# First stage of a hybrid encoder block in another written order: meta tokens' norm ahead, norm row by a selector made on chip, first tile scaled in halves

## The chip, the core and the metric

The kernel runs on one core of a Trainium2 chip. The time is the device's time of one launch, in microseconds (us); the kernel before was run three times for it. A core has engines with a queue each, and every queue is worked off in order: TensorE (PE: matmuls, with PEld its loads of the stationary operand), VectorE (DVE), ScalarE (ACT), GpSimd (POOL) and SyncE (SP). Engines wait for each other by semaphores only. DMAs are issued from the queues of SP and ACT; an issue holds its place in that queue until what it waits for is there.

## The reference, cut to what matters

1024 tokens of 1024 float32 values, with 16 learned meta tokens ahead of them, go through one layer: a norm, a wide projection into eight parts, a pooling branch and a gated linear attention, both joined by gates, then a squared-ReLU MLP and a last norm. The change lies in the norm and in the part `v` of the projection.

```python
def rmsnorm(x, g):
    return x * lax.rsqrt(jnp.mean(x * x, axis=-1, keepdims=True) + EPS) * g

h = jnp.concatenate([meta, x], axis=1)
z = jnp.einsum('bld,dn->bln', rmsnorm(h, norm_mix[l]), w_in)
a, q, k, v, r, lr, ga, gb = jnp.split(z, IN_SPLITS, axis=-1)
```

## The kernel before, in words

**Arithmetic.** Most products are made of three float32r matmuls: each operand is split into a high part (ACT writes a rounded copy) and a low part (DVE subtracts it), and hi x hi, hi x lo and lo x hi go into one PSUM bank (`mm3`, lines 276 to 281). Each of the many products therefore needs an ACT and a DVE step on both of its operands.

**The first stage** (`first_stage`, with the functions that it defines) takes the tokens in tiles of 128 (t = 0 to 7; t = 8 is the 16 meta tokens). For each tile:

- `load` brings it in (`xs`, four slots; an SP DMA).
- `square`, `log`, `exp` (ACT) and `root` (four small DVE steps) make one factor for each token from the sum of squares.
- `scale` (line 498, DVE, 128x1024) multiplies by that factor and by the norm row `gB` into `us`. A `scale` also issues the load of a later tile. `gB` holds the 1024 values of `norm_mix` on all 128 partitions; it is made on chip before any `scale`.
- `turn t j` (line 513, PE) transposes half j of the tile, four 128x128 blocks, into a PSUM bank, `b_sc` and `b_ms` by turns. The two banks called `b_sc` are halves of one tile, `sc`.
- `hi` (line 526, ACT) and `lo` (line 529, DVE) split that half into `th` and `tl`; `keep` (line 519, ACT) copies it unsplit into `xr`. For tile 0, `keep` comes first and `hi`, `lo` read `xr`.
- `high i j` (line 541, ACT) and `low i j` (line 545, DVE) split half j of the weights' columns i = 0 or 1, that lie in `raw` and go to `vw`. `ask` issues the load of the next half of weights (SP); it waits until the old one in that buffer has been read. `low20` is a small piece of 16 columns.
- `value i t j` (PE) multiplies half j of tile t with weights i: twelve matmuls of 256 columns (272 for i = 1). Only for (0, 0) it uses the unsplit `xr` and raw weights, four float32 matmuls (line 382). `out i t` (line 399, ACT) takes the sum from its bank and stores it.
- `meta8` transposes the scaled meta tokens `um` (line 272, PE) and splits them; `value080` to `value181` use them.

On ACT, DVE, SP and PE of this stage, the order is written out by hand, as a list of words in `ORDER_1` (lines 418 to 430): `square0 log0 exp0 ...` calls `square(0)`, `log(0)` and so on, and each call's instructions go to the end of their engines' queues. PE's order is kept to the end of the program.

**Ahead of the list** stand the DMAs and the norm row. `ident` (a unit matrix) is loaded from ACT's queue; `norm_mix` follows it into eight partitions of `row`, which DVE has zeroed (line 449). Two `warm` matmuls of 128x512 on zeros come first on PE (line 467, each as two passes), then eight matmuls of 128 columns that use a column of `ident`, broadcast, to spread the eight pieces of the row over all partitions (line 474), DVE copies the two banks to `gB` (line 477), and three more `warm` follow.

**After the first stage** come the small gate projection (`lr_turn`, which needs `lrtok` of all tiles), pooling, the attention, the output projection and the MLP, the last two with seven products instead of eight for each 2x2 of blocks. Sums of blocks of `xr` for them (lines 701 to 705, DVE) already stand in DVE's queue at the end of the first stage. `W1` is the ring of weight blocks of the later projections; `W1.ask` (the word `wait00`) issues its two first loads, `W1.split` (`first1`, `first2`) splits them (lines 84 and 85).

Of the kernel before, what the change touches and what calls it, by code (L numbers as in the profile page):

```python
# [11 lines left out]
ALU = mybir.AluOpType  # L12
AX = mybir.AxisListType

P = 128
D = 1024
SEQ = 1024
META = 16
KT = D // P
# [103 lines left out]
def kernel(  # L123
# [3 lines left out]
    nc = tc.nc  # L127
    x = x[0]
    out = out[0]
# [73 lines left out]
    TH, TL = [], []  # L203
# [161 lines left out]
    def halves():  # L365
        return [slice(h * HALF, (h + 1) * HALF) for h in range(2)]
# [2 lines left out]

    v_bank = {}  # L370

    def v_half(i, t, j):
# [4 lines left out]
        if j == 0:  # L377
            v_bank[i, t] = bank("mm")
        b = v_bank[i, t][:n, :w]
        if (i, t) == (0, 0):  # L380
            for k in range(4 * j, 4 * j + 4):
                pe.matmul(b, S["xr"][:, k, :P], S["vraw"][j][:, k % 4], start=k == 0, stop=k == KT - 1)
        else:
            mm3(
                b, 4, lambda k: (TH[half][:, 4 * j + k, at : at + n], TL[half][:, 4 * j + k, at : at + n]),
                lambda k: (vw[:, 0, 4 * j + k], vw[:, 1, 4 * j + k]), first=j == 0, last=j == 1,
            )

    def v_out(i, t):
# [12 lines left out]
    def lr_turn():  # L402
# [13 lines left out]


    ORDER_1 = """
        square0 log0 exp0 root0 square1 scale0 log1 exp1 turn00 high00 root1 turn01 keep00 scale1 keep01 value000
        hi00 low00 ask10 high01 turn10 square2 low01 turn11 value001 ask11 hi10 log2 lo10 exp2 square3 root2 value010 scale2  # L420
        hi11 hi01 log3 lo11 out00 turn20 exp3 turn21 hi20 root3 value011 high10 lo20 scale3 high20 hi21 low20 value020 keep10
        keep11 lo01 square4 lo21 turn30 turn31 lo00 hi30 value021 log4 lo30 hi31 keep30 lo31 value030 exp4 keep20 out01
        root4 high11 low10 value031 out02 keep21 square5 scale4 value100 low11 wait00 log5 out03 exp5 turn40 turn41 root5
        value101 hi40 scale5 lo40 hi41 lo41 keep31 keep40 value110 out10 keep41 square6 log6 exp6 value111 value120
        out11 turn50 turn51 root6 hi50 scale6 lo50 hi51 lo51 value121 out12 value040 keep50 keep51 first1 value041 out04
        value130 turn60 turn61 hi60 lo60 hi61 lo61 value131 out13 square7 log7 exp7 root7 scale7 value050 keep60 keep61
        value051 out05 value140 turn70 turn71 hi70 lo70 hi71 lo71 value141 out14 square8 log8 exp8 root8 scale8 value060
        keep70 keep71 value061 out06 first2 value150 meta8 value151 out15 value070 value071 out07 value160 value161 out16
        value170 value171 out17 value080 value081 out08 value180 value181 out18
    """  # L430

    def first_stage(xs, us, xm, um, lrraw):
# [7 lines left out]
        def load(t):  # L440
            nc.sync.dma_start(xs[:, t % 4], x[t * P : (t + 1) * P, :])
# [8 lines left out]
        nc.scalar.dma_start(row[:KT], norm_mix.rearrange("(k c) -> k c", c=P))  # L450
        act.preload_act_table_set("natural_log_exp_and_others")
        pool.memset(blank, 0.0)
# [12 lines left out]
        def warm(n, cols=HALF):  # L465
            for _ in range(n):
                pe.matmul(bank("ms")[:, :cols], blank[:, HALF:], blank[:, :cols], start=True, stop=True)

        warm(2)
        for h, c in enumerate(halves()):  # L470
            b = bank("mm")
            for i in range(4):
                k = 4 * h + i
                pe.matmul(
                    b[:, i * P : (i + 1) * P], ident[:, k : k + 1].broadcast_to([P, P]), row, start=True, stop=True
                )
            dve.tensor_copy(gB[:, c], b)
        warm(3)

        def square(t):  # L480
            act.activation(um[: P if t < 8 else META], x_in(t), ACT.Square, accum_out=cell(3, t))
# [7 lines left out]
        def root(t):  # L489
# [3 lines left out]
            dve.tensor_scalar(m, m, -0.5, 1.5, ALU.mult, ALU.add)  # L493
            dve.tensor_tensor(ss, y, m, ALU.mult)

        def scale(t):
            u = x_out(t)
            dve.scalar_tensor_tensor(u, x_in(t), cell(3, t), gB[: u.shape[0]], ALU.mult, ALU.mult)
            if t == 0:
                load(4)  # L500
# [42 lines left out]
        def low(i, j):  # L543
            whole, hi, lo = parts(i, j)
            dve.tensor_tensor(lo, whole, f32(hi), ALU.subtract)

        does = dict(
            wait=lambda i, j: W1.ask(),
            square=square, log=log, exp=exp, root=root, scale=scale, turn=turn, keep=keep, hi=hi, lo=lo, high=high,
            low=low, ask=ask, value=v_half, out=v_out, first=W1.split, meta=lambda t: transposed(um[:META], 0, 0),  # L550
        )
        for word in ORDER_1.split():
            name = word.rstrip("0123456789")
# [1166 lines left out]
```

## Time and profile before

| | |
|---|---|
| median of 3 runs | 1215.61 us (1215.55 to 1216.33) |
| the profiled execution's own time | 1216.04 us |
| its span on the core | 1214.3 us |
| PE busy | 1198.8 us (99%) |
| DVE busy | 841.8 us (69%) |
| ACT busy | 573.3 us (47%) |
| POOL busy | 77.7 us (6%) |

The profile is of one execution of its own; about 1.7 us of that execution's time lie around the span. Times in rows are microseconds from the span's start. A row of the timeline has start, duration, engine, line, operation, what it writes `<-` what it reads, shape, and how many instructions it merges; in brackets the idle time of the engine ahead of it and what ended it. Matmuls are pipelined: the next one starts before the one before has ended, so that an end is the start plus a little more than the pace. `xN` of a float32 matmul counts its passes, two for each instruction. A row of windows has for each engine the busy time and the number of instructions in that stretch.

### The profile page before, as it was taken

To read this page: it belongs to the slowest core of one execution; us is meant where nothing else is said; L and a number is where in the kernel's file an instruction comes from. 1 tells how busy PE (TensorE), PEld (TensorE's weight loads), DVE (VectorE), ACT (ScalarE), POOL (GpSimd) and SP (SyncE) were. 2 spreads that over 40 slices of the span, in tenths; PEclk is the share of its full clock that TensorE was granted. 3 is DMA by queue.
4 is the path that set the end of the run, shared out by engine and by line. 5 is a ranking of instruction groups with operands and counts; after the bars stand their busy time and mean duration, and the time that the engine had idled before them with its cause. 6 is when DMAs were issued, how large, how long until landed. Compare 5 with 4: busy or idle time off the path is not lost.

```text
span 1214.3 us, 18327 instructions
## 1 busy us (share of the span) xinstructions
PE 1198.8 (99%) x6775; PEld 993.0 (82%) x6775; DVE 841.8 (69%) x1386; ACT 573.3 (47%) x1013; POOL 77.7 (6%) x97
## 2 busy tenths in 40 slices
PE   9999999999999999999999999999999999999997
PEld 7999877877778887888788888888888888888886
DVE  7646567575777669726887667676675887887786
ACT  7537444444456224305655545454554444444544
POOL 0000053323230000000000000000000000000000
PEclk9999999999999999999999999999999999999999
DMA  8214243434338967812245444454479973333532
GB/s 241 78 53 130 89 120 123 145 124 141 119 111 287 336 219 254 302 40 87 87 144 169 146 157 157 130 171 145 162 245 307 353 235 100 96 97 94 174 96 87
DMA packets 151385, 192.79 MB, mean 159 GB/s; under 512 B 12216, under 2 KB 86256, under 8 KB 151296
## 3 DMA queue, kind: packets, MB, share of 16 engines
q1 hardware_dynamic: 151136, 191.56, 49.1%
q8 instruction: 53, 0.87, 0.3%
q14 instruction: 36, 0.29, 0.1%
q10 hardware_dynamic: 160, 0.07, 0.0%
HBM read 128.66 MB, written 62.93 MB: 158 GB/s over the span
## 4 chain that ended last, share of the span: by engine, by line
PE 88%; DVE 5%; DMA 3%; issue 2%; ACT 1%; POOL 0%; SPq 0%; DVEq 0%; ACTq 0%; POOLq 0%
PE b_mm L279 7%; PE b_mm L280 7%; PE b_mm L281 7%; PE b_y L279 6%; PE b_y L280 6%; PE b_y L281 6%; PE b_oa L279 5%; PE b_oa L281 5%; PE b_oa L280 5%; PE b_z L279 4%; PE b_z L280 4%; PE b_z L281 4%; PE b_sc L279 4%; PE b_ob L279 4%; PE b_ob L280 4%; PE b_ob L281 4%
## 5 line engine op out<-in xcount | busy, mean ns | idle before, releaser
L768 ACT ACTIVATE w1h<-raw 128x512 fp32r<-128x512 f32 x106 | 65.9, 623 | 57.8 <-PE b_y L280 23.2
L769 DVE TENSOR_TENSOR w1l<-raw,w1h 128x512 fp32r<-128x512 f32 x106 | 72.5, 685 | 20.4 <-ACT w1h L768 20.4
L279 PE MATMUL b_sc<-th,w1h 128*128 128x512 f32 x216 | 85.6, 396 | 0.6 <-ACT u2p L1503 0.6
L279 PE MATMUL b_z<-th,w1h 128*128 128x512 f32 x216 | 85.3, 395 | 0.5 <-DVE c L887 0.3
L280 PE MATMUL b_sc<-tl,w1h 128*128 128x512 f32 x216 | 84.9, 393 | 0.0
L280 PE MATMUL b_z<-tl,w1h 128*128 128x512 f32 x216 | 84.2, 390 | 0.4 <-DVE tl L1389 0.4
L281 PE MATMUL b_sc<-th,w1l 128*128 128x512 f32 x216 | 84.4, 391 | 0.0
L768 ACT ACTIVATE w1h<-fs 128x512 fp32r<-128x512 f32 x81 | 51.1, 631 | 70.3 <-PE b_y L280 33.3
L281 PE MATMUL b_z<-th,w1l 128*128 128x512 f32 x216 | 84.1, 389 | 0.0
L769 DVE TENSOR_TENSOR w1l<-fs,w1h 128x512 fp32r<-128x512 f32 x81 | 56.9, 703 | 26.6 <-ACT w1h L768 26.5
L279 PE MATMUL b_mm<-th,w1h 128*128 128x512 f32 (+1 forms) x208 | 72.0, 346 | 0.0
L281 PE MATMUL b_mm<-th,w1l 128*128 128x512 f32 (+1 forms) x208 | 71.1, 342 | 0.0
L280 PE MATMUL b_mm<-tl,w1h 128*128 128x512 f32 (+1 forms) x208 | 71.0, 342 | 0.0
L768 ACT ACTIVATE w1h<-bt 128x512 fp32r<-128x512 f32 x46 | 29.1, 632 | 70.9 <-issue 43.9
L1579 DVE TENSOR_TENSOR bt<-w,w 128x512 f32<-128x512 f32 x80 | 54.7, 683 | 2.5 <-DMA w<-in_w_ff_dram 2.5
L279 PE MATMUL b_mm<-wo,th 128*128 128x512 f32 x128 | 50.3, 393 | 0.0
L281 PE MATMUL b_mm<-wo,tl 128*128 128x512 f32 x128 | 49.9, 390 | 0.0
L280 PE MATMUL b_mm<-wo,th 128*128 128x512 f32 x128 | 49.8, 389 | 0.0
L279 PE MATMUL b_y<-wo,w1h 128*128 128x512 f32 x128 | 49.8, 389 | 0.0
L280 PE MATMUL b_y<-wo,w1h 128*128 128x512 f32 x128 | 49.8, 389 | 0.0
L281 PE MATMUL b_y<-wo,w1l 128*128 128x512 f32 x128 | 49.8, 389 | 0.0
L769 DVE TENSOR_TENSOR w1l<-bt,w1h 128x512 fp32r<-128x512 f32 x46 | 31.8, 691 | 25.6 <-ACT w1h L768 25.6
(420 smaller groups left out, 3322.8 us busy)
## 6 DMA issues: line engine op xcount, KB each, us to landing
hf_dram<-h SPq DMA_DIRECT2D x112, 256.0 KB, 2.1
raw<-hf_dram SPq DMA_DIRECT2D x112, 256.0 KB, 2.7
w<-in_w_ff_dram SPq DMA_DIRECT2D x64, 256.0 KB, 4.6
raw<-in_w_in_dram SPq DMA_DIRECT2D x22, 512.0 KB, 4.5
raw<-in_w_ff_dram SPq DMA_DIRECT2D x16, 512.0 KB, 4.1
rawx<-in_w_ff_dram SPq DMA_DIRECT2D x16, 512.0 KB, 4.1
rawp<-in_w_in_dram SPq DMA_DIRECT2D x10, 512.0 KB, 4.4
xs<-in_x_dram SPq DMA_DIRECT2D x8, 512.0 KB, 4.9
```

The lines of the kernel that those rows point to most:

```text
L279: pe.matmul(ps, ah, bh, start=first and i == 0, stop=False, skip_group_check=more)
L280: pe.matmul(ps, ah, bl, start=False, stop=False, skip_group_check=more)
L281: pe.matmul(ps, al, bh, start=False, stop=last and i == n - 1, skip_group_check=more)
L768: act.activation(hi, a, ACT.Copy)
L769: dve.tensor_tensor(lo, a, f32(hi), ALU.subtract)
L1579: dve.tensor_tensor(bt, w, S["w2"][q[3:]][:, i], ALU.add if q[2] == "+" else ALU.subtract)
```

## The change

Five things are changed, all in the first stage.

1. **Norm row.** `norm_mix` is loaded as four rows of 256 into partitions 0, 32, 64 and 96 of a zeroed row buffer of 256 columns. Instead of a column of `ident`, four selectors of 128x128 are made on chip: DVE zeroes `ones` (128x512) and sets one partition of each to 1. Four matmuls of 256 columns (two `spread`) take the place of the eight of 128; `copy0` and `copy1` (DVE) are words of the list now. The DMA of `ident` moves from the head of ACT's queue to the third place of SP's, behind the first two tiles of tokens and ahead of the weights.
2. **Warm matmuls.** One 128x512 ahead of the spreads instead of two; four of 128x128 (`warm4`) behind `exp1` instead of three of 128x512.
3. **Tile 0** is scaled in two halves (`half00`, `half01`, 128x512 each).
4. **Quarters.** `bit i t q` multiplies a quarter (two of the eight blocks); `value011` and `value021` are written as `bit012 bit013` and `bit022 bit023`, with other work between them.
5. **The list.** Among other moves: `copy1 half00 half01` stand ahead of `root1`; `lo11` stands ahead of `root2 scale2`; `keep10 keep11` ahead of `hi20`; `lo21` ahead of `scale3`; `hi00 hi01 lo00 lo01` and `low11` ahead of `scale4`; `wait00` comes after `out10`; `square8 log8 exp8 root8 scale8`, the norm of the meta tokens, moves from behind `out14` to the words around `scale7`.

Three places, as each engine's queue has them. First ACT from the `log` of tile 3 on (line 484 before, 491 now): `th<-b_sc` and `th<-b_ms` are `hi` of tile 2, `th<-xr` is `hi` of tile 0, `xr<-b_sc` and `xr<-b_ms` the `keep` of tiles 1 and 2. Before:

```order
L484 ACTIVATE small<-small 128x1
L399 ACTIVATE vo<-b_mm 128x256
L487 ACTIVATE small<-small 128x1
L526 ACTIVATE th_132<-b_sc 128x4x128
L541 ACTIVATE vw_190<-raw_116 128x4x256
L541 ACTIVATE vw_190<-lrraw 128x8x16
L526 ACTIVATE th_132<-b_ms 128x4x128
L519 ACTIVATE xr<-b_sc 128x4x128
L519 ACTIVATE xr<-b_ms 128x4x128
L481 ACTIVATE um,small<-xs 128x1024
```

Now:

```order
L491 ACTIVATE small<-small 128x1
L494 ACTIVATE small<-small 128x1
L399 ACTIVATE vo<-b_mm 128x256
L530 ACTIVATE xr<-b_sc 128x4x128
L530 ACTIVATE xr<-b_ms 128x4x128
L537 ACTIVATE th_132<-b_sc 128x4x128
L537 ACTIVATE th_132<-b_ms 128x4x128
L399 ACTIVATE vo<-b_mm 128x256
L552 ACTIVATE vw_190<-raw_116 128x4x256
L552 ACTIVATE vw_190<-lrraw 128x8x16
```

Two `keep` stand between the bookkeeping of tile 3 and `hi20` now, where before `hi20` came at once and the two `keep` of tile 1 stood four rows below it. In the program the first of these `keep` waits for the last transpose of `turn20`, because both halves of `b_sc` are one tile.

Second DVE from the low half of `lrraw` to the scaling of tile 4 (`us<-xs`, line 498 before, 511 now); `tl` rows are `lo`, `vw_190` rows are `low`. Before:

```order
L545 TENSOR_TENSOR vw_190<-lrraw,vw_190 128x8x16
L529 TENSOR_TENSOR tl_136<-xr,th_132 128x4x128
L529 TENSOR_TENSOR tl_136<-b_ms,th_132 128x4x128
L529 TENSOR_TENSOR tl_136<-xr,th_132 128x4x128
L529 TENSOR_TENSOR tl_136<-b_sc,th_132 128x4x128
L529 TENSOR_TENSOR tl_136<-b_ms,th_132 128x4x128
L491 TENSOR_SCALAR small<-small 128x1
L492 SCALAR_TENSOR_TENSOR small<-small 128x1
L493 TENSOR_SCALAR small<-small 128x1
L494 TENSOR_TENSOR small<-small 128x1
L545 TENSOR_TENSOR vw_190<-raw_116,vw_190 128x4x256
L498 SCALAR_TENSOR_TENSOR us<-xs,small,gB 128x1024
```

Now:

```order
L556 TENSOR_TENSOR vw_190<-lrraw,vw_190 128x8x16
L556 TENSOR_TENSOR vw_190<-raw_116,vw_190 128x4x256
L540 TENSOR_TENSOR tl_136<-b_sc,th_132 128x4x128
L540 TENSOR_TENSOR tl_136<-b_ms,th_132 128x4x128
L540 TENSOR_TENSOR tl_136<-xr,th_132 128x4x128 x2
L498 TENSOR_SCALAR small<-small 128x1
L499 SCALAR_TENSOR_TENSOR small<-small 128x1
L500 TENSOR_SCALAR small<-small 128x1
L501 TENSOR_TENSOR small<-small 128x1
L556 TENSOR_TENSOR vw_190<-raw_120,vw_190 128x4x256
L511 SCALAR_TENSOR_TENSOR us<-xs,small,gB 128x1024
```

Now `low11` (`raw_120`) stands ahead of the scaling of tile 4; before it stood behind it.

Third DVE around the norm of the meta tokens (shapes with 16 partitions). Before:

```order
L529 TENSOR_TENSOR tl_144<-b_ms,th_140 128x4x128
L394 COPY lrtok<-b_mm 128x16
L491 TENSOR_SCALAR small<-small 16x1
L492 SCALAR_TENSOR_TENSOR small<-small 16x1
L493 TENSOR_SCALAR small<-small 16x1
L494 TENSOR_TENSOR small<-small 16x1
L701 TENSOR_TENSOR xr<-xr 128x4x512
L498 SCALAR_TENSOR_TENSOR um<-xm,small,gB 16x1024
```

Now:

```order
L498 TENSOR_SCALAR small<-small 16x1
L499 SCALAR_TENSOR_TENSOR small<-small 16x1
L500 TENSOR_SCALAR small<-small 16x1
L501 TENSOR_TENSOR small<-small 16x1
L511 SCALAR_TENSOR_TENSOR um<-xm,small,gB 16x1024
L540 TENSOR_TENSOR tl_144<-b_sc,th_140 128x4x128
L540 TENSOR_TENSOR tl_144<-b_ms,th_140 128x4x128
L394 COPY lrtok<-b_mm 128x16
L716 TENSOR_TENSOR xr<-xr 128x4x512
```

The norm of the meta tokens is done ahead of the `lo` of tile 7, and the large sum on `xr` (line 701 before, 716 now) no longer stands between its small steps and its scaling.

From the large sums on, every engine has the same instructions in the same order in both programs, but for the second of these sums on DVE, which now stands ahead of the split of a `W1` block and of the meta tokens' `lo`.

The diff, cut to its core (lines further down move by 15):

```diff
-        row = us[:, 2, :P]
-        nc.scalar.dma_start(ident, ident_in)
+        row, ones = us[:, 2, : 2 * P], us[:, 2, 2 * P : 6 * P].rearrange("p (q c) -> p q c", q=4)
         dve.memset(row, 0.0)
-        nc.scalar.dma_start(row[:KT], norm_mix.rearrange("(k c) -> k c", c=P))
+        dve.memset(ones, 0.0)
+        nc.scalar.dma_start(
+            row.rearrange("(q r) c -> q r c", r=32)[:, 0], norm_mix.rearrange("(q c) -> q c", q=4)
+        )
+        for q in range(4):
+            dve.memset(ones[32 * q : 32 * q + 1, q], 1.0)
...
         load(0)
         load(1)
+        nc.sync.dma_start(ident, ident_in)
...
-        warm(2)
-        for h, c in enumerate(halves()):
-            b = bank("mm")
-            for i in range(4):
-                k = 4 * h + i
-                pe.matmul(
-                    b[:, i * P : (i + 1) * P], ident[:, k : k + 1].broadcast_to([P, P]), row, start=True, stop=True
-                )
-            dve.tensor_copy(gB[:, c], b)
-        warm(3)
+        warm(1)
+        rows = []
+
+        def spread(h):
+            rows.append(bank("mm"))
+            for i in range(2):
+                c = slice(2 * i * P, 2 * (i + 1) * P)
+                pe.matmul(rows[h][:, c], ones[:, 2 * h + i], row, start=True, stop=True)
+
+        def copy(h):
+            dve.tensor_copy(gB[:, halves()[h]], rows[h])
...
+        def half(t, h):
+            c = halves()[h]
+            dve.scalar_tensor_tensor(x_out(t)[:, c], x_in(t)[:, c], cell(3, t), gB[:, c], ALU.mult, ALU.mult)
+            if h:
+                load(t + 4)
...
+            warm=lambda n: warm(n, P),
+            value=lambda i, t, j: v_part(i, t, range(4 * j, 4 * j + 4)),
+            bit=lambda i, t, q: v_part(i, t, range(2 * q, 2 * q + 2)),
```

The list begins so now (one line of the fourteen):

```python
        spread0 spread1 copy0 square0 log0 exp0 root0 copy1 half00 half01 square1 log1 exp1 root1 warm4 turn00 turn01
```

More of the change, by code (lines that the diff above doesn't have):

```diff
@@ L380, in v_half @@
         if (i, t) == (0, 0):
[L381 to L386 removed]
+            for k in ks:
+                pe.matmul(b, S["xr"][:, k, :P], S["vraw"][k // 4][:, k % 4], start=k == 0, stop=k == KT - 1)
+        else:
+            mm3(
+                b, len(ks), lambda k: (TH[half][:, ks[k], at : at + n], TL[half][:, ks[k], at : at + n]),
+                lambda k: (vw[:, 0, ks[k]], vw[:, 1, ks[k]]), first=ks.start == 0, last=ks.stop == KT,
             )
@@ L418 @@
     ORDER_1 = """
[L419 to L427, printed above, removed]
@@ L428 @@
-        keep70 keep71 value061 out06 first2 value150 meta8 value151 out15 value070 value071 out07 value160 value161 out16
-        value170 value171 out17 value080 value081 out08 value180 value181 out18
+        spread0 spread1 copy0 square0 log0 exp0 root0 copy1 half00 half01 square1 log1 exp1 root1 warm4 turn00 turn01
+        keep00 scale1 high00 keep01 value000 low00 ask10 high01 low01 turn10 turn11 hi10 value001 ask11 square2 lo10
+        hi11 log2 exp2 lo11 root2 value010 bit012 scale2 square3 log3 exp3 root3 out00 turn20 turn21 bit013 keep10
@@ new lines @@
+        keep11 hi20 lo20 hi21 lo21 scale3 value020 out01 high10 high20 low20 low10 bit022 turn30 turn31 bit023 hi30
+        lo30 hi31 lo31 hi00 hi01 value030 lo00 lo01 square4 log4 exp4 high11 root4 low11 scale4 keep20 out02 keep21
+        value031 keep30 value100 out03 keep31 square5 log5 exp5 turn40 turn41 root5 value101 hi40 scale5 lo40 hi41
+        lo41 value110 out10 wait00 keep40 keep41 square6 log6 exp6 value111 value120 out11 turn50 turn51 root6 hi50
+        scale6 lo50 hi51 lo51 value121 out12 value040 keep50 keep51 first1 value041 out04 value130 turn60 turn61 hi60
```

15 lines of the change are left out of this document (9 added, 6 removed).

## Prediction

> **What bounds the kernel now.** I read the page first, then busy time by stretches of the first stage, then PE's waits there.
>
> ```profile
> span 1214.3 us, 18327 instructions
> PE 1198.8 (99%) x6775; PEld 993.0 (82%) x6775; DVE 841.8 (69%) x1386; ACT 573.3 (47%) x1013; POOL 77.7 (6%) x97
> ...
> 0.00:11.01 11.01, 9.14 (x26) 4.78 (x27) 3.50 (x10) 5.42 (x10) 1.12 (x7) 1.00 0.86 293
> 11.01:18.64 7.63, 7.11 (x44) 6.21 (x44) 6.81 (x14) 6.91 (x16) 0.00 (x0) 1.00 0.84 224
> 18.64:29.04 10.40, 10.40 (x89) 10.40 (x89) 9.80 (x20) 9.76 (x23) 0.81 (x1) 1.00 0.81 214
> 29.04:56.60 27.56, 27.56 (x226) 27.14 (x224) 15.83 (x35) 18.69 (x43) 0.00 (x0) 1.00 0.30 88
> 56.60:58.48 1.88, 0.00 (x0) 0.00 (x1) 1.88 (x3) 0.00 (x0) 0.00 (x0) 1.00 0.17 56
> 58.48:1214.30 1155.82, 1144.64 (x6393) 944.51 (x6393) 803.94 (x1309) 532.56 (x924) 75.74 (x89) 1.00 0.49 158
> ```
>
> PE is busy 1198.8 of 1214.3 us, so only two things can move the end: time in which PE stands still, and when the dense part begins. Until 11.01 PE runs nothing that counts (zeros, and the norm row). Then it is busy but for half a microsecond up to 18.64 (`turn20`), without a gap from 18.64 to 56.60, stands still for 1.88 us, and goes on. In the row 18.64:29.04 (`turn20` to `turn40`), DVE is busy 9.80 and ACT 9.76 of 10.40 us: PE is the bound there with almost nothing to spare. From 29.04 on DVE has room (15.83 of 27.56).
>
> ```profile
> PE b_ms L272 <- DVE um L498: 1.9, 1, 1.9
> PE b_sc L513 <- DVE us L498: 0.6, 2, 0.3
> ```
>
> PE's one long wait is for the scaled meta tokens.
>
> **The meta tokens' norm (term 1).**
>
> ```profile
> 52.74 1.04 ACT L481 ACTIVATE um<-xm 16x1024 f32<-16x1024 f32 x1
> 54.96 2.28 DVE L701 TENSOR_TENSOR xr<-xr 128x2048 f32<-128x2048 f32 x1
> 56.31 0.29 PE L281 MATMUL b_mm<-vw,tl 128*128 128x272 f32 x1
> 57.16 1.27 DVE L498 SCALAR_TENSOR_TENSOR um<-xm,small,gB 16x1024 f32<-16x1024 f32 x1
> 58.48 0.66 PE L272 MATMUL b_ms<-ident,um 16*128 16x16 f32 x8 [1.88 <-DVE um L498]
> ```
>
> The scaling started only at 57.16, behind a sum of 2.28 us on `xr`; PE's last matmul ahead of it began at 56.31, the transposes at 58.48. Now this norm is done a whole tile earlier, so the stand goes: 1.88 us by the row of idle time, 2.05 us by the starts (58.48 - 56.31, less the pace of 0.12 that 27.56 us for 226 matmuls gives). I take **-2.0**. What it moves: 1.0 us of ACT and 1.3 us of DVE ahead of tile 7's `hi` and `lo`, in a stretch of 27.56 us where ACT has 8.9 and DVE 11.7 us to spare. With this wait gone, nothing else on the path to `meta8` is late there: its transposes follow `value150` at once.
>
> **The opening (term 2).** The rows that give its terms:
>
> ```profile
> 1.19 0.58 ACTq L450 DMA_DIRECT2D us<-in_norm_mix_dram  x1
> 1.46 3.78 PE L467 MATMUL b_ms<-xr 128*128 128x512 f32 x4 [1.46 <-POOL xr L452]
> 4.86 1.06 ACT L481 ACTIVATE um<-xs 128x1024 f32<-128x1024 f32 x1 [1.77 <-DMA xs<-in_x_dram]
> 5.35 2.79 PE L474 MATMUL b_mm<-us,ident 128*128 128x128 f32 x16
> 6.43 0.20 ACT L487 ACTIVATE small<-small 128x1 f32<-128x1 f32 x1
> 7.28 0.69 DVE L477 COPY gB<-b_mm 128x512 f32<-128x512 f32 x1 [6.25 <-PE b_mm L474]
> 7.97 2.74 PE L467 MATMUL b_ms<-xr 128*128 128x512 f32 x6
> 8.78 0.14 DVE L491 TENSOR_SCALAR small<-small 128x1 f32<-128x1 f32 x1
> 9.67 1.28 DVE L498 SCALAR_TENSOR_TENSOR us<-xs,small,gB 128x1024 f32<-128x1024 f32 x1
> 11.01 0.66 PE L513 MATMUL b_sc<-ident,us 128*128 128x128 f32 x4 [0.30 <-DVE us L498]
> ...
> wgu<-in_w_gate_up_dram SPq DMA_DIRECT2D x3, 16.0 KB, 2.4
> ...
> small<-in_b_gate_dram SPq DMA_DIRECT2D x1, 1.0 KB, 3.5
> ```
>
> *The row's landing* is not shown alone. It is issued at about 1.2 as before. Small loads took 2.4 us (`wgu`, rows of 1 KB as here) and 3.5 (`b_gate`, single values): 3.6 to 4.7. The upper bound is 5.3, where the norm matmuls started before, behind `ident`'s 128 rows in the same queue. I take 4.0, nearer to `wgu`. [...]
>
> *Spreads.* A pass of 512 columns takes 0.9 us in the row at 1.46 (3.78 for four) and 0.46 in the one at 7.97 (2.74 for six): PE's pace doubled in between, though the clock column of the windows (third from the right) reads 1.00 throughout. At the slow pace a pass of 256 columns is 0.45; each spread is two matmuls, four passes, 1.8 us, so that the second ends at 4.0 + 3.6 = 7.6, a little sooner where the pace doubles on the way.
>
> *DVE.* `exp0` ends at 6.63; `copy0` (0.69 from 5.9) and `root0` are done by 7.5. `copy1` from 7.6, start to start 0.6; `half00` from 8.2 (0.64 to 0.69, half of 1.28 or like a 128x512 copy), `turn00` at **8.9** against 11.01. `half01` from 8.8, `root1` (four small steps, 0.89 from 8.78 to 9.67) from 9.4, `scale1` from 10.3.
>
> Covered: the memsets (DVE idles 6.25 us ahead of its first copy), `warm4` (eight passes of 128 columns at a quarter of 0.46, 0.9 us, ending at 8.5, ahead of 8.9), `ident` on SP (issued near 1.7; a landing like the others' 4 to 5 us is 3 us ahead of `turn00`; it holds back the weight loads by one issue and 64 KB, some 0.4 us, which `high00`, behind `turn00` now, does not feel). Without that last cover, `value000` would be late by the same 0.4.
>
> **Where the gain goes (term 3).**
>
> ```profile
> 11.76 1.28 DVE L498 SCALAR_TENSOR_TENSOR us<-xs,small,gB 128x1024 f32<-128x1024 f32 x1
> ...
> 17.30 1.28 DVE L498 SCALAR_TENSOR_TENSOR us<-xs,small,gB 128x1024 f32<-128x1024 f32 x1
> ...
> 18.64 0.66 PE L513 MATMUL b_sc<-ident,us 128*128 128x128 f32 x4 [0.27 <-DVE us L498]
> 19.34 0.60 ACT L526 ACTIVATE th<-b_sc 128x512 fp32r<-128x512 f32 x1 [0.56 <-PE b_sc L513]
> 19.97 0.69 DVE L529 TENSOR_TENSOR tl<-b_sc,th 128x512 fp32r<-128x512 f32 x1
> 20.58 1.27 DVE L498 SCALAR_TENSOR_TENSOR us<-xs,small,gB 128x1024 f32<-128x1024 f32 x1
> 21.46 0.60 ACT L519 ACTIVATE xr<-b_sc 128x512 f32<-128x512 f32 x1
> 21.93 0.61 ACT L519 ACTIVATE xr<-b_ms 128x512 f32<-128x512 f32 x1
> ...
> 26.15 1.22 DVE L545 TENSOR_TENSOR vw<-raw,vw 128x1024 fp32r<-128x1024 f32 x1
> 27.28 1.53 DVE L498 SCALAR_TENSOR_TENSOR us<-xs,small,gB 128x1024 f32<-128x1024 f32 x1
> ...
> 29.04 0.60 PE L513 MATMUL b_sc<-ident,us 128*128 128x128 f32 x4
> ```
>
> From `scale1` to `scale2` DVE took 17.30 - 11.76 = 5.54 us; now `lo11` lies in it too, 0.61 (19.97 to 20.58): 6.15. `scale2` starts at 10.3 + 6.15 = 16.45 and `turn20`, 1.34 behind as before, at 17.8: **-0.85**, of the 2.1 that `turn00` won. The rest is `lo11` and the factor of tile 1, which starts behind both halves. The quarters (`bit`) are the same matmuls in another place and cost nothing of their own.
>
> From `turn20` to `turn40`, before, 10.40 us. Now: `hi20` came 0.70 after `turn20`; two `keep` at 0.47 each (21.46, 21.93) stand ahead of it, and the first must wait for `turn20`. So `lo20` comes at +0.70 + 0.94 + 0.63 = +2.3, DVE idle meanwhile. Counting from `lo20`: `lo20`, `lo21` (0.61 each), `scale3`, and `turn30` at +2.55. `hi30` +3.25, `lo30` +3.9 (DVE has done `low20`, `low10` by then); `lo31 lo00 lo01` to +6.3. ACT goes `hi30 hi31 hi00 hi01` (0.47 each) to +5.15, then `square4` to `exp4` done 1.77 later (4.86 to 6.63): +6.9; `high11` (1.07, as `low11`'s partner) to +7.9; `low11` +7.9 to +9.05 (1.13 from 26.15 to 27.28); `scale4` and `turn40` 1.34 later: +10.4. Together 12.7 against 10.40: **+2.3**. PE had exactly 10.40 us of work on that leg and now has less, since `bit012` is done ahead of it: it stands for 2.3 us at least.
>
> From `turn40` to the meta tokens PE's work is the same and gapless. The first loads of `W1`, now behind `out10`, are asked for some 8 us later than before; their first product is far off:
>
> ```profile
> 76.67 0.37 PE L279 MATMUL b_mm<-th,w1h 128*128 128x264 f32 x1
> ```
>
>
> **Sum:** -0.85 + 2.3 - 2.0 = **-0.55 us** on 1216.04, 1215.5. That execution is 0.43 above the median; against the median 1215.61 I forecast **1215.1**. Bounds: row at 3.6 gives -1.15 in place of -0.85, at 5.3 `copy1` starts at 8.2 and it is -0.25; term 3 is +1.35 if the `keep` found no wait, +2.55 if `scale4` takes 1.53 as at 27.28; term 1 is -1.9 to -2.05. Ends: -1.85 to +0.4, so 1213.75 to 1216.0. A measurement of this kernel can tell about 0.2%, 2.4 us, from no change.
>
> **Rivals.**
> *A, faster: the leg from `turn20` to `turn40` is not longer.* Then -0.85 - 2.0 = -2.85, 1212.8. For it: ACT is ahead at 17.8 and might hide the `keep`. Against it: the wait for `turn20` stands in the program, and DVE's 9.80 of 10.40 leaves no room. Chance 0.09.
> *B, slower: the clock doubles late.* Place: PE up to value000. Before, PE had worked on zeros and the row for 3.8 to 6.5 us when its pace doubled (from 1.46 to between 5.24, the end of the four passes, and 7.97); now two passes end at 3.3 and PE pauses until the row lands. Counted from 4.0 anew, the step comes between 7.8, which costs nothing, and 10.5: then `warm4` ends at 9.4 instead of 8.5, half a microsecond after `turn00` could start, and each `turn` of tile 0 (0.44 for its four) takes twice as long, partly beside ACT's work: +0.5 to +0.95, taken as +0.7, 1215.8. Every microsecond after that costs about half of one. The sum is slower than before from a step at about 10 on, and by 0.2% only from about 15 (+3.0). Against it: PE works from 4.0 to 7.6 without a gap. Chance 0.12, 0.07 of it near 1215.8 and 0.05 at 1217 or more. By the Trainium skill's page "TensorE: Matmul & The Clock Gate" (Part 1) the clock stays at half until one free-running window of about 3.4 us was busy. By that rule the pause costs either nothing or one whole window, an estimate of 10.3 for the step and 1215.8 for the time; the trace of before agrees with one step after such a stretch.
> *C, the meta gain is given back later:* two sums of 2.28 us now stand ahead of the split of a `W1` block on DVE. If PE waited for it, -0.85 + 2.3 = +1.45, 1217.1. Against it: that split can only start behind the meta tokens' scaling (57.16 + 1.27 before) and is as long as the 1.22 at 26.15, while the first product stands at 76.67: 17 us of room for 2.28. Chance 0.05.
>
> **Numbers.** Forecast 0.74. Within its own ends and with B's first case 0.81 lie in 1213.5 to 1216.5, widened by the runs' own spread of 0.8. Faster by over 0.2%: A, 0.09. Slower by over 0.2%: B's far case, 0.04. Within: 0.87.
>
> **What would show it.** Right: `turn00` near 8.9, `turn20` near 17.8, `turn40` near 30.5, DVE idle ahead of `lo20`, PE standing about 3 us between 17 and 31, none ahead of the line 272 transposes, which come near 57.9. Wrong: `turn40` at or before 29; passes of 0.43 for 256 columns still after 8; a new long wait of PE after 58.

## The result, and the profile after

The changed kernel takes **1218.47 us** (median of 11 runs, 1218.12 to 1219.38) beside 1215.92 us for the kernel before (11 runs on the same chip): a ratio of 1.0019 (95% interval 1.0011 to 1.0027), 2.55 us slower. The forecast was 1215.1 with 1213.5 to 1216.5. Run once more, later, it took 1218.84 beside 1216.27: 1.0021 (1.0012 to 1.0030).

The profiled execution took 1219.38 us. The head of its page:

```profile
span 1217.6 us, 18321 instructions
PE 1198.3 (98%) x6767; PEld 993.5 (82%) x6767; DVE 843.2 (69%) x1392; ACT 573.6 (47%) x1013; POOL 77.2 (6%) x97
```

Its busy time by the stretches that the prediction used (start to `turn00`, to `turn20`, to `turn40`, to the meta tokens' transposes, to the end); the columns are those of the rows of before, first the length, then busy time of PE, PEld, DVE, ACT, POOL:

```profile
0.00:10.83 10.83, 7.33 (x19) 5.04 (x19) 4.19 (x15) 4.46 (x9) 1.12 (x7) 1.00 0.83 293
10.83:19.74 8.91, 8.05 (x52) 7.01 (x51) 8.02 (x16) 7.30 (x15) 0.00 (x0) 1.00 0.84 222
19.74:32.69 12.95, 10.64 (x83) 9.84 (x83) 10.15 (x19) 10.70 (x23) 0.51 (x1) 1.00 0.57 155
32.69:60.17 27.48, 27.46 (x225) 27.09 (x225) 17.17 (x36) 18.70 (x43) 0.00 (x0) 1.00 0.32 89
60.17:1217.59 1157.42, 1144.82 (x6394) 944.51 (x6393) 803.72 (x1309) 532.41 (x924) 75.62 (x89) 1.00 0.49 158
```

PE's busy time is the same within half a microsecond (1198.3 against 1198.8). What changed is time in which it stands. The first stretch is 10.83 against 11.01, where 8.9 was forecast. The second and third are 1.28 and 2.55 us longer than before, the fourth is 1.96 shorter (27.48 against 29.44). All four together end 1.69 later than before. The last is 1.60 longer (1157.42 against 1155.82); 0.72 of that stands at one line near 345 us (runs 7 and 9), and the rest, 0.88, is about what two profiles of one kernel differ by there (0.6 and 0.8 in the repeats below).

PE's waits in the first 62 us of the changed kernel:

```profile
PE b_mm L482 <- DMA us<-in_norm_mix_dram: 2.0, 1, 2.0
PE b_sc L524 <- ACT xr L530: 1.5, 1, 1.5
PE b_ms L473 <- POOL xr L457: 1.5, 1, 1.5
PE b_sc L524 <- DVE us L511: 0.7, 1, 0.7
PE b_mm L279 <- ACT th L537: 0.5, 1, 0.5
PE b_mm L281 <- DVE tl L540: 0.2, 1, 0.2
```

The 1.9 us ahead of line 272 are gone. In their place stand 0.7 us ahead of `turn20`, 0.5 and 0.2 behind it, 1.5 ahead of `turn40`, and 2.0 us for the norm row, ahead of the spreads (the 1.5 of line 473 are the start, as before). The 1.5 us are put down to ACT's `keep` on `xr`, but the rows around `turn40` name another:

```profile
31.20 0.61 ACT L530 ACTIVATE xr<-b_sc 128x512 f32<-128x512 f32 x1
31.26 1.28 DVE L511 SCALAR_TENSOR_TENSOR us<-xs,small,gB 128x1024 f32<-128x1024 f32 x1
31.68 0.40 ACT L399 ACTIVATE vo<-b_mm 128x256 f32<-128x256 f32 x1
31.94 0.63 ACT L530 ACTIVATE xr<-b_ms 128x512 f32<-128x512 f32 x1
...
32.69 0.30 PE L524 MATMUL b_sc<-ident,us 128*128 128x128 f32 x1 [1.53 <-ACT xr L530]
```

The copy out of `b_sc` was done at 31.81; the scaling of tile 4 ended at 32.54, 0.15 ahead of `turn40`. The last `keep` ended at nearly the same moment, and the view named it. (In a run below the same `turn40` starts 0.71 ahead of that `keep`'s end.)

The opening, in order of time:

```profile
1.17 1.09 ACTq L451 DMA_DIRECT2D us<-in_norm_mix_dram  x1
...
1.46 2.07 PE L473 MATMUL b_ms<-xr 128*128 128x512 f32 x2 [1.46 <-POOL xr L457]
...
5.57 3.75 PE L482 MATMUL b_mm<-us 128*128 128x256 f32 x8 [2.04 <-DMA us<-in_norm_mix_dram]
...
7.66 0.69 DVE L485 COPY gB<-b_mm 128x512 f32<-128x512 f32 x1 [5.00 <-PE b_mm L482]
...
9.12 1.92 PE L473 MATMUL b_ms<-xr 128*128 128x128 f32 x8
...
9.37 0.69 DVE L485 COPY gB<-b_mm 128x512 f32<-128x512 f32 x1 [0.24 <-PE b_mm L482]
9.97 1.40 DVE L505 SCALAR_TENSOR_TENSOR us<-xs,small,gB 128x512 f32<-128x512 f32 x2
...
10.83 0.77 PE L524 MATMUL b_sc<-ident,us 128*128 128x128 f32 x4
```

The issue of the row's DMA takes 1.09 us where it took 0.58, and the spreads begin at 5.57. Their eight passes take 3.55 us to the start of the next row, 0.44 each: the slow pace. `warm4` runs at the slow pace too (0.21 for 128 columns) and ends where `turn00` starts.

### The profile page after: what moved, and what is told of

Its sections match the earlier page's. It is cut to its first block, busy times and chain, and to the rows that moved or that the text cites. A ratio compares the mean times of both kernels' runs of the same rounds, so it can differ in the third digit from the quotient of the medians.

```text
span 1217.6 us, 18321 instructions
## 1 busy us (share of the span) xinstructions
PE 1198.3 (98%) x6767; PEld 993.5 (82%) x6767; DVE 843.2 (69%) x1392; ACT 573.6 (47%) x1013; POOL 77.2 (6%) x97
## 4 chain that ended last, share of the span: by engine, by line
PE 88%; DVE 5%; ACT 3%; DMA 2%; issue 2%; POOL 0%; SPq 0%; DVEq 0%; ACTq 0%; POOLq 0%
PE b_mm L279 7%; PE b_mm L281 7%; PE b_mm L280 7%; PE b_y L279 6%; PE b_y L280 6%; PE b_y L281 6%; PE b_oa L281 5%; PE b_oa L279 5%; PE b_oa L280 5%; PE b_z L279 4%; PE b_z L280 4%; PE b_z L281 4%; PE b_sc L279 4%; PE b_ob L281 4%; PE b_ob L280 4%; PE b_ob L279 4%
```

## The experiments

Each kernel ran beside the kernel before on one chip. "Spread" is the start of the first matmul on the norm row; "doubles" is the moment at which PE's pace doubles, from the trace's entries of the granted clock, which the lengths of the passes confirm; the legs are `turn00` to `turn20`, `turn20` to `turn40`, `turn40` to the meta tokens' transposes; "PE matmuls" is the page's count, in which a float32 matmul is two; "store" is the time from issue to the last landing of a store near 330 us (`gi_dram<-gi`, below).

| kernel | median | before | ratio (95%) | spread | doubles | `turn00` | legs | PE matmuls | store |
|---|---|---|---|---|---|---|---|---|---|
| before | 1215.92 | | | 5.35 | 6.95 | 11.01 | 7.63, 10.40, 29.44 | 6775 | 6.6 |
| before, again | 1216.37 (one) | | | 5.09 | 6.66 | 10.73 | 7.63, 10.39, 29.50 | 6775 | 6.6 |
| after | 1218.47 | 1215.92 | 1.0019 (1.0011 to 1.0027) | 5.57 | 11.16 | 10.83 | 8.91, 12.95, 27.48 | 6767 | 7.6 |
| after, again | 1218.84 | 1216.27 | 1.0021 (1.0012 to 1.0030) | 6.03 | 10.79 | 11.22 | 8.80, 12.94, 27.51 | 6767 | 7.6 |
| meta norm alone | 1213.43 | 1216.35 | 0.998 (0.9971 to 0.9988) | 5.29 | 5.97 | 10.51 | 7.63, 10.42, 27.56 | 6775 | 6.6 |
| two warm | 1217.88 | 1216.35 | 1.0015 (1.0006 to 1.0024) | 5.86 | 9.71 | 11.05 | 8.80, 12.94, 27.50 | 6769 | 7.5 |
| `keep` back | 1217.50 | 1216.35 | 1.0012 (1.0004 to 1.0021) | 6.03 | 9.56 | 11.18 | 8.80, 11.16, 27.76 | 6767 | 7.2 |
| new opening, old list | 1214.12 | 1216.35 | 0.9987 (0.9978 to 0.9996) | 5.92 | 5.07 | 9.84 | 7.87, 10.95, 27.49 | 6769 | 7.5 |
| old opening, new list | 1217.62 | 1216.46 | 1.0005 (0.9996 to 1.0014) | 5.33 | 7.65 | 11.34 | 8.79, 12.96, 27.49 | 6775 | 7.0 |
| pause filled | 1217.38 | 1216.46 | 1.0004 (0.9995 to 1.0013) | 5.90 | 6.33 | 10.03 | 8.80, 12.95, 27.52 | 6773 | 7.6 |
| `ident` on ACT | 1219.03 | 1216.46 | 1.0017 (1.0009 to 1.0026) | 6.09 | 9.60 | 11.23 | 8.79, 12.95, 27.50 | 6767 | 7.7 |
| row adjacent | 1217.15 (one) | | | 4.77 | 9.49 | 9.97 | 8.80, 12.95, 27.50 | 6767 | 7.1 |
| pause filled, matmuls as before | 1216.93 | 1216.27 | 1.0006 (0.9997 to 1.0015) | 6.05 | 7.32 | 10.59 | 8.80, 12.94, 27.50 | 6775 | 6.4 |
| new opening filled, old list | 1213.79 | 1216.27 | 0.998 (0.9971 to 0.9989) | 6.20 | 5.25 | 10.12 | 7.86, 10.90, 27.52 | 6775 | 6.5 |

The theory at the start of the runs: the opening won nothing, since the row landed late and PE's pace doubled late; the new list is longer by its own words. The rivals stand with each run.

**1. Meta norm alone**, in the kernel before:

```diff
-out13 square7 log7 exp7 root7 scale7 value050 ... out14 square8 log8 exp8 root8 scale8 value060
+out13 square7 log7 exp7 square8 log8 exp8 root7 scale7 root8 value050 keep60 keep61 scale8 value051 ... out14 value060
```

> The kernel before, with one part of the change alone: the meta tokens' norm (square8 to scale8) stands around scale7. Theory: PE's wait ahead of the line 272 transposes goes and nothing else moves; transposes near 56.4 (58.48 less 2.0), lr transposes (line 409) near 73.8, and the 2.0 us last to the end: about 1213.9 beside 1215.9 for before. Rival: the gain is swallowed behind line 409, where the new kernel lost 1.6 us more than at line 409; then the time stays within 0.5 us of before.

The transposes started at 56.12 and the time fell by 2.4 us (0.2%, 0.12 to 0.29%). PE's longest wait after `turn00` is 0.3:

```profile
PE b_sc L513 <- DVE small L491: 0.3, 1, 0.3
PE b_sc L513 <- DVE us L498: 0.3, 1, 0.3
PE b_mm L382 <- ACT xr L519: 0.2, 1, 0.2
```

The part is worth what term 1 said, and it lasts to the end. The rest of the change therefore costs about 5 us (2.55 + 2.4).

**2. Two warm matmuls** ahead of the spreads:

```diff
-        warm(1)
+        warm(2)
```

> The changed kernel with two warm matmuls of 128x512 ahead of the spreads, as before, in place of one; nothing else differs. Theory (PE's pace): with no pause of PE between 3.5 and 5.6, the pace doubles near 7 as in before and not near 11.2; the second spread ends about 0.9 us sooner (four passes at 0.22 in place of 0.43), turn00 comes 0.4 to 0.9 us sooner than 10.83, turn20 0.6 to 1.2 us sooner than 19.7, and the time is 0.6 to 1.2 us less than that of the changed kernel (1217.3 to 1217.9). Rival (only the landing of the norm row counts, and DVE is the bound up to turn20): the pace doubles at 7, but turn20 stays within 0.3 us of 19.7 and the time within 0.3 us of the changed kernel's.

The run didn't bring about what it was to test. The two warm matmuls ended at 5.24, the row came 0.62 later, and the pace doubled only at 9.71:

```profile
1.46 3.78 PE L473 MATMUL b_ms<-xr 128*128 128x512 f32 x4 [1.46 <-POOL xr L457]
...
5.86 3.75 PE L482 MATMUL b_mm<-us 128*128 128x256 f32 x8 [0.62 <-DMA us<-in_norm_mix_dram]
```

It says that a pause of 0.6 us is enough to put the doubling off, and left the price open.

**3. The two `keep` and `low11` back** in the changed list:

```diff
-bit013 keep10 keep11 hi20 lo20 hi21 lo21 scale3 ... root4 low11 scale4
+bit013 hi20 lo20 hi21 lo21 keep10 keep11 scale3 ... root4 scale4 low11
```

> The changed kernel with keep10 and keep11 behind hi20 lo20 hi21 lo21, and low11 behind scale4; the opening as changed. Theory (these words lengthen the leg): turn20 stays at 19.7, turn20 to turn40 falls from 13.0 to 11.0 (0.94 for the two copies, 1.13 for low11), PE's stand ahead of turn40 falls from 1.7 to under 0.5, and 1 to 2 us are left at the meta transposes: 1216.5 to 1217.5. Rival: the leg is long because DVE is short of time whatever stands first (9.8 of 10.4 us busy before): then the copies only move the wait, turn40 stays within 0.5 us of 32.7 and the time within 0.4 us of the changed kernel's.

The leg fell from 12.95 to 11.16, as the theory said; about 0.26 of that was given back in the next leg. By the ratios the time fell by 0.07 to 0.09%, some 1 us, though the intervals of the two kernels overlap. The rows around `turn40` in this kernel:

```profile
29.19 1.28 DVE L511 SCALAR_TENSOR_TENSOR us<-xs,small,gB 128x1024 f32<-128x1024 f32 x1
...
30.48 0.60 ACT L530 ACTIVATE xr<-b_sc 128x512 f32<-128x512 f32 x1
...
31.14 0.66 PE L524 MATMUL b_sc<-ident,us 128*128 128x128 f32 x4
...
31.22 0.63 ACT L530 ACTIVATE xr<-b_ms 128x512 f32<-128x512 f32 x1
```

Here the scaling of tile 4 ended at 30.47 and `turn40` started at 31.14, right behind the copy out of `b_sc` (31.08) and 0.71 ahead of the last `keep`'s end (31.22 + 0.63 = 31.85). So the wait in the changed kernel was for the scaling.

**4. New opening, old list.** Norm row, halves and meta norm as changed, `warm(2)`, and from `turn00` on the words of before:

```diff
-        warm(1)
+        warm(2)
...
-exp1 root1 warm4 turn00 turn01 keep00 scale1 high00 keep01 value000
+exp1 warm4 turn00 high00 root1 turn01 keep00 scale1 keep01 value000
...
```

> The changed kernel's norm row, halves of tile 0 and meta norm, two warm matmuls of 128x512, and from turn00 on the words in the order of before. Theory: turn00 comes 0.6 to 1.5 us sooner than the 11.01 of before, turn20 to turn40 takes 10.4 again, and the meta wait is gone: 0.5 us or more under the kernel before with the meta norm alone, 1212.9 to 1213.5. Rival: what turn00 wins is lost by turn20, as DVE sets the pace from scale1 to scale2 (5.5 us): then the time is that of before with the meta norm alone, about 1213.9.

`turn00` came at 9.84, since by chance the pace doubled at 5.07, ahead of the pause. But `turn40` is at 28.66 and the meta transposes at 56.15, as with the meta norm alone (28.56 and 56.12): the first leg gave back 0.24 (7.87 against 7.63), the second 0.53. The rival was right for the time: what `turn00` wins in this order is lost again by `turn40`.

**5. Old opening, new list.** The norm row, warm matmuls and whole `scale0` of before, the changed words from `turn00` on:

```diff
-spread0 spread1 copy0 square0 log0 exp0 root0 copy1 half00 half01 square1 log1 exp1 root1 warm4 turn00 turn01
+square0 log0 exp0 root0 scale0 square1 log1 exp1 root1 turn00 turn01
```

> The opening of before (norm row by columns of ident, ident on ACT's queue, three plus two warm matmuls, tile 0 scaled in one piece) with the changed list from turn00 on. Theory (the list loses, the opening gained nothing): turn00 at 10.5 to 11.0 as in before, turn00 to turn20 8.2 to 8.9 (one piece of scaling gives back up to 0.6), turn20 to turn40 13.0, turn40 to the meta transposes 27.5, against 7.6, 10.4 and 29.4 before: 1.3 to 1.9 us over before. Rival: the legs are long in the changed kernel only because its opening is late against the loads; then turn20 to turn40 is under 11 and the time at or under that of before.

Its stretches from `turn00` on:

```profile
11.34:20.13 8.79, 7.82 (x50) 6.92 (x51) 7.49 (x15) 7.29 (x15) 0.00 (x0) 1.00 0.78 220
20.13:33.09 12.96, 10.64 (x83) 9.86 (x83) 9.95 (x19) 10.72 (x24) 0.55 (x1) 1.00 0.56 152
33.09:60.58 27.49, 27.47 (x225) 27.10 (x225) 17.16 (x36) 18.64 (x42) 0.00 (x0) 1.00 0.31 90
```

The legs are those of the changed kernel to a tenth, so they belong to the list, not to the opening ahead of it: 8.79 + 12.96 + 27.49 against 7.63 + 10.40 + 29.44, 1.77 us more. `turn00` came later than expected, at 11.34, with the pace doubling at 7.65. The medians differ by 1.16 and the ratio by 0.05% with an interval from -0.04 to 0.14% (up to 1.7 us): the times by themselves do not show the sign, the trace does.

**6. The pause filled:**

```diff
-        warm(1)
+        warm(2)
+        warm(2, P)
```

> The changed kernel with two warm matmuls of 128x512 and two of 128x128 ahead of the spreads, so that PE works from 1.46 until the norm row is there. Theory (the pace doubles at the end of one stretch of fixed length, about 3.4 us by the trace's clock records, in which PE never stood): the step comes between 4.9 and 8.3 and not at 9.6 to 11.2, the eight passes of the spreads take 2 to 3 us in place of 3.7, turn00 comes near 10.0 and turn20 near 18.9, and the time is 0.5 to 1.0 us under the changed kernel's. Rival (the pace depends on the row's work itself, or comes at any time): the step lies after 9 again, the spreads take 3.7, turn00 is at 11 or later.

```profile
1.46 4.64 PE L473 MATMUL b_ms<-xr 128*128 128x512 f32 x8 [1.46 <-POOL xr L457]
5.90 2.17 PE L483 MATMUL b_mm<-us 128*128 128x256 f32 x8
7.91 1.05 PE L473 MATMUL b_ms<-xr 128*128 128x128 f32 x8
10.03 0.66 PE L525 MATMUL b_sc<-ident,us 128*128 128x128 f32 x4 [1.06 <-DVE us L506]
```

The pace doubled at 6.33, the spreads took 2.0 us from start to start, and `turn00` came at 10.03. Against the second run of the changed kernel, whose spreads began 0.13 later, that is 1.06 us for the pace alone (11.22 - 10.03 - 0.13). The ratio fell from 1.0019 and 1.0021 to 1.0004, some 1.8 to 2.1 us, more than the 0.5 to 1.0 expected; the intervals overlap a little, and the profile shows no cause for the excess.

**7. `ident` back on ACT's queue.** In the changed kernel a store near 330 us takes a microsecond longer than before, and PE stands for it at line 1004 near 345. The first guess at the cause was the DMA of `ident`, which the change had moved:

```diff
-        nc.sync.dma_start(ident, ident_in)
...
+        nc.scalar.dma_start(ident, ident_in)
```

> The changed kernel with the DMA of ident back on ACT's queue, behind the norm row's, so that SP's queue has the order of before. Theory (moving this DMA to SP shifted which transfers share a DMA engine, and with it the store gi_dram near 330, whose last sixteenth landed 1.2 us behind the others): that store's parts land within 0.5 us of each other again, PE's stand of 0.8 ahead of line 1004 near 345 is gone, and the time is about 0.6 us under the changed kernel's. Rival: the store is late by what runs beside it in this list; then the last part is still over 1 us late and the time within 0.3 us of the changed kernel's. The opening should not change by more than 0.3 us.

The theory fell: the store took 7.7 us again and the time was 1.0017 of before.

**8. The row in adjacent partitions:**

```diff
-            row.rearrange("(q r) c -> q r c", r=32)[:, 0], norm_mix.rearrange("(q c) -> q c", q=4)
+            row[:4], norm_mix.rearrange("(q c) -> q c", q=4)
```

> The changed kernel with the four pieces of the norm row in partitions 0 to 3 in place of 0, 32, 64 and 96; the selectors are left as they are, so that three of the four pieces are not spread (the norm row is partly zero). One look at the row's DMA. Theory (the stride over partitions makes the issue longer, and the landing follows the issue's end by 3.2 to 3.6): the issue takes 0.6 as in before and not 1.1, and the row lands near 5.0. Rival: rows of 1 KB, or the tiles of x that move ahead of it, set the landing: it stays at 5.4 to 5.9.

```profile
1.17 0.54 ACTq L451 DMA_DIRECT2D us<-in_norm_mix_dram  x1
...
4.77 3.75 PE L482 MATMUL b_mm<-us 128*128 128x256 f32 x8 [1.24 <-DMA us<-in_norm_mix_dram]
```

The issue takes 0.54, and the spreads start at 4.77 against 5.57 to 6.20 in the nine other profiles with the new row, which have it in partitions 0, 32, 64 and 96. `turn00` is at 9.97 although the pace doubled only at 9.49. This kernel leaves three of the four pieces of the row unspread; the instructions are otherwise the same. So the partitions, not the size of the pieces, cost half a microsecond at the issue. The spreads came sooner by more than that, 0.8 to 1.4 us; that the partitions cost this too rests on this one profile.

**9. The pause filled, and as many matmuls as before** (five in place of four behind `exp1`):

```diff
-exp1 root1 warm4 turn00
+exp1 root1 warm5 turn00
```

> The kernel with the pause filled (two warm matmuls of 128x512 and two of 128x128 ahead of the spreads), and five in place of four of 128x128 behind exp1, so that PE has as many matmuls as before (6775 in the trace; the changed kernel has 6767). Theory: a DMA packet of 16 KB of instructions comes at a place in PE's stream that the number of its instructions sets; 0.5 us after the issue of the store gi_dram near 330 before, 2 to 5 us after it in the kernels with fewer matmuls, there among the store's own packets, so that one of its 16 parts lands about 1.2 us late and PE stands 0.6 us at line 1004 near 345. With 6775 matmuls the packet is at +0.5 again, the last part lands at +6.5 to +7.0 and not at +7.2 to +7.7, line 1004 starts at +14.9, and the time is about 0.6 us less than without the fifth warm matmul. Rival: the store is late for another reason; then its last part is at +7.2 or later again, wherever the packet is, and the time stays within 0.3 us.

What SP waited for behind the store, in the changed kernel and in this one:

```profile
SPq L1021 <- DMA gi_dram<-gi: 5.5, 1, 5.5
```

```profile
SPq L1022 <- DMA gi_dram<-gi: 4.2, 1, 4.2
```

The packets and MB of each DMA queue while the store's data move, from 0.7 us behind its issue to its end, in the same order:

```profile
q1 hardware_dynamic: 1283, 1.55, 75.1%
q8 instruction: 1, 0.02, 0.9%
q14 instruction: 1, 0.01, 0.3%
```

```profile
q1 hardware_dynamic: 1299, 1.56, 88.6%
q14 instruction: 1, 0.01, 0.3%
```

The trace of the kernel before has 53 packets of 16 KB in `q8`, one for about every 256 of PE's 13550 weight loads and matmuls, so they are taken to be PE's instructions. In the changed kernel one of them lies in that stretch; here it lies 0.25 us behind the store's issue, ahead of its data, and the store lands 6.4 us after its issue and not 7.6. Line 1004 starts 14.93 us after the store's issue here and 15.65 in the changed kernel, where PE shows the wait:

```profile
PE b_gs L1004 <- ACT gi L1026: 0.6, 1, 0.6
```

All fourteen profiles agree. With 6775 matmuls the packet lies 0.25 to 0.6 us behind the issue, the store takes 6.4 to 7.0, and the matmuls at that line start at +14.93, in six of six. With 6767 to 6773 the packet lies 2.2 to 5.2 us behind it, the store takes 7.1 to 7.7, and they start at +15.1 to +15.8, in eight of eight. The price, 0.2 to 0.9 us and 0.72 in the changed kernel, is read from these starts. The times do not show it by themselves: this run's ratio is 1.0006 against 1.0004 without the fifth matmul, with a `turn00` later by 0.56 in its profile. The spans do: from the meta tokens' transposes to the end of the span, the six profiles with 6775 matmuls take 1155.6 to 1156.4 us (mean 1155.96), the eight others 1156.1 to 1157.4 (mean 1156.64), so about 0.7 us lasts to the end, though the two ranges overlap.

**10. The new opening filled, old list**, with 6775 matmuls and the meta norm moved; against the kernel of run 4:

```diff
         warm(2)
+        warm(2, P)
...
-exp1 warm4 turn00
+exp1 warm5 turn00
```

> The new norm row and halves with the pause filled and 6775 matmuls, the words from turn00 on in the order of before, and the meta norm moved: the parts of the change that gained, without those that lost. Theory: turn00 near 9.9, turn20 near 17.8, turn40 near 28.5, meta transposes near 56.0 and no late store: 0.3 to 0.8 us under before with the meta norm alone, so 2.7 to 3.3 us under before. Rival: the loads and DVE give the opening's gain back by turn40 (as in the run with the order of before and the pause left in, whose leg from turn20 to turn40 took 10.95): then 2.0 to 2.5 under before, no better than the meta norm alone.

1213.79, a ratio of 0.998 (0.9971 to 0.9989), the same as the meta norm alone. The rival was right: `turn00` at 10.12 against 10.51, but the legs are 0.23 and 0.48 longer and `turn40` is at 28.88 against 28.56. Both beat the kernel before and the changed one; the simpler edit, the meta norm alone, is as good.

**11 and 12. Both kernels again:**

> The changed kernel once more, for its times beside the others on one chip and a second profile. Theory: the legs turn00 to turn20, turn20 to turn40 and turn40 to the meta transposes repeat within 0.15 us (8.9, 12.95, 27.5), turn00 itself moves by up to 0.7 us with the moment at which the pace doubles (9.0 to 12.4) and with the row's landing (5.4 to 5.9), and the time is 2 to 2.6 us over before. Rival: the legs themselves vary by half a microsecond, and the readings from single profiles do not hold.

> The kernel before once more, for a second profile. Theory: turn00 differs from 11.01 with the moment at which the pace doubles (4.9 to 8.3; half a microsecond for each), while the legs repeat within 0.15 us (7.6, 10.4, 29.4), and the store gi_dram lands whole at about +6.6. Rival: legs or store vary as much as the kernels differ.

The legs repeat within 0.11 us, as the theory said. `turn00` moves by 0.28 and 0.39, and in both pairs this is mostly the start of the spreads, which moves the same way by 0.26 and 0.46. So single profiles carry the legs, and `turn00` has to be read together with the start of the spreads and the moment of doubling.

## Why the prediction was wrong

**Term 1, right.** -2.0 forecast; the leg to the meta transposes is 1.96 to 1.99 us shorter, and alone the part is worth 2.4 us by the ratio.

**Term 3, right.** +2.3 forecast, 12.7 for the leg; measured 12.95, in every kernel with these words. PE stands 0.7 us ahead of `turn20` and 2.2 from there up to `turn40`, where about 3 were foretold in all. Its steps hold too: `lo20`, with DVE idle ahead of it, starts 2.30 us behind `turn20` (2.3 forecast), and `turn40` 10.65 behind `lo20` (10.4):

```profile
22.04 0.69 DVE L540 TENSOR_TENSOR tl<-b_sc,th 128x512 fp32r<-128x512 f32 x1 [1.58 <-ACT th L537]
```

Undoing the words that the term named took 1.79 back.

**Term 2, wrong, and it is the largest miss.** It had two halves. From `turn00` to `turn20` it gave 8.9 us (17.8 less 8.9); measured 8.91 and 8.80. The step that failed is the row's landing: "I take 4.0, nearer to `wgu`", with "The upper bound is 5.3, where the norm matmuls started before". The spreads began at 5.57 and 6.03, so 4.40 and 4.86 us behind the start of the issue, where 2.8 had been taken. Of the 1.6 to 2.0 us that this is more, 0.5 is the issue itself: the prediction costed the bytes of the new row and the place of its issue, not its length, which is 1.09 over four partitions that lie 32 apart and was 0.58 before. So the row of before was no bound. The other 1.1 to 1.5 us lie behind the issue's end, and their cause is not shown. A row of before that was nearer than `wgu` in time and queue comes close to it: the load of `ident`, issued from ACT's queue just ahead of the norm row, landed 4.3 us after its issue.

```profile
ident<-in_ident_dram ACTq DMA_DIRECT2D x1, 64.0 KB, 4.3
```

The working of the bound also took an early doubling for granted: at the slow pace, which the sum itself uses, `copy1` starts at 5.3 + 3.6 = 8.9 and not at 8.2. From the spreads on the working holds nearly as written: `copy1` starts 3.8 us after them (3.6 forecast), the first half 0.6 behind that, and `turn00` another 0.86 and 0.79 (0.7). `turn00` came at 10.83 and 11.22 in place of 8.9: an error of 1.9 to 2.3 us.

**Rival B happened, at a smaller price.** Its mechanism was this one: two passes, a pause until the row is there, the doubling counted anew. It set 7.8 to 10.5 for the step with a row at 4.0; with spreads from 5.57 and 6.03 on the step came at 11.16 and 10.79. Its sign, passes of 0.43 for 256 columns after 8, is there: the spreads' row runs from 5.57 to 9.32. The chance of 0.12 was too low, because one mis-sized landing feeds both: a late row delays the spreads and lengthens the pause. Its price, 0.5 to 0.95 us, was counted as the excess over a forecast that already took the spreads at the slow pace. Of that excess about 0.2 us is seen: with the doubling at 11.16, `turn00` starts 0.86 behind the first half and the first leg is 8.91, against 0.79 and 8.80 with the doubling at 10.79. The whole of what an early doubling is worth is the 1.06 us of run 6.

**Not foreseen at all:** the 0.7 us of the store near 330 us. The prediction put no cost on what lies behind the first stage. What lies there has the same instructions as before, but PE's stream is 8 matmuls shorter ahead of them, and by the fourteen profiles of run 9 that moved a packet of instructions into a store. Of the signs that the prediction named, it is the new wait of PE after 58.

**The sum, with what was measured:** the opening +0.2 (10.83 and 11.22 against 11.01 and 10.73), the leg to `turn20` +1.2, to `turn40` +2.55, to the meta transposes -2.0, the store +0.7: +2.65, against 2.55 and 2.57 by the medians. The forecast had -2.1, +1.3, +2.3, -2.0 and 0. That the sum meets the medians to 0.1 is partly luck, since the last stretch alone differs by 0.6 to 0.8 between two profiles of one kernel.

Rivals A and C did not occur: the leg is longer, and nothing of the meta gain is given back up to line 409 (17.29 us after the transposes, 17.28 before).

## What to carry to other kernels

Cost a moved or reshaped DMA by its issue as well: a destination that strides over partitions is another instruction than the one whose row is at hand, and such a row bounds nothing. In this case the load nearest in time and queue sized the landing better than the one of like rows did. Where one late event feeds two terms, such as a landing that also sets how long TensorE pauses, give the two one chance together and let the range hold both. A written order could be read from the profile before to a quarter of a microsecond, leg by leg, and an opening can be won and still be worth nothing where the stretch behind it is full on DVE and ACT.

## What the runs showed of the hardware that was not expected

- **TensorE's pace doubles at the end of a window, not after an amount of work.** In all fourteen profiles it came 3.5 to 6.2 us after PE had begun to work without a pause. From the doubling to the fall at the end the clock entries last 1201.49 or 1204.91 us, which differ by 3.41 and are 352 and 353 times 3.4133 us. Counted back from the doubling by such windows, PE stood 0.11 us at most in the last one and 0.6 us or more in the one before it, in all fourteen. A pause of 0.69 us just behind the doubling (run 4) did not bring the slow pace back. This is the rule of the Trainium skill's page "TensorE: Matmul & The Clock Gate" (Part 1), a free-running window of 3413 ns that must be busy, and the traces agree with it. Since the window does not start with the kernel, the opening moves from run to run with the same instructions: in the four profiles with the opening of before, the pace doubled at 5.97, 6.66, 6.95 and 7.65, and from the start of the spreads to `turn00` it took 5.22, 5.64, 5.66 and 6.01 us.
- **An issue of four pieces took 0.54 us into partitions 0 to 3 and 1.09 to 1.11 into partitions 0, 32, 64 and 96.**
- **A fetch of instructions seems to delay data.** With a 16 KB packet of PE's instructions among a store's packets, the last sixteenth of the store landed 0.7 to 1.4 us behind the one before it (eight profiles); with the packet ahead of the data it was 0.33 us at most (six). The Trainium skill's page "Runtime: NRT & Kernel Launch" (Instruction fetch mechanics) tells of such blocks and calls the cost of crossing from one to the next mostly hidden; of data that move beside a block it says nothing, and here that cost about 0.7 us. That the packet and the late part went through the same DMA engine is inferred from the fourteen profiles, not seen in an entry of its own.
